# Latent attention: the values' low halves moved into one 128-column operand, the 64th added on VectorE

## The chip, the cores and the metric

One Trainium2 chip, one core. The metric is the device time of one execution in microseconds (us), median of several runs. The engines are TensorE (PE; its weight loads are shown apart as PEld), VectorE (DVE), ScalarE (ACT), GpSimd (POOL) and SyncE (SP), which issues the DMAs.

## The reference

Two layers on x of 1 x 512 x 1024 float32. In each, one projection of the normed input gives the inputs of three branches and three gates; the branches are projected, gated, summed and projected once more; a gated MLP with a depthwise convolution follows. The change is in branch A, the multi-head latent attention (MLA), with a few edits elsewhere:

```python
kv = (rms_norm(c_kv, kv_norm_g) @ w_ukv).reshape(b, s, MLA_HEADS, MLA_NOPE + MLA_V)
k_nope, v = kv[..., :MLA_NOPE], kv[..., MLA_NOPE:]      # MLA_V = 64, MLA_HEADS = 8
...
sc = jnp.einsum('bqgrd,bkgd->bgrqk', qi, k) * scale
p = jax.nn.softmax(sc, axis=-1)
return jnp.einsum('bgrqk,bkgv->bqgrv', p, v)
```

Branch B is a grouped-query attention (GQA) with 8 query and 2 key/value heads, branch C a multi-scale mean pooling.

## The kernel before, in words

**Numbers.** Every float32 operand of a matmul is held as a high and a low half of type float32r: `hi` is the rounded value (a copy on ACT or DVE), `lo` the difference (a subtraction on DVE or POOL). `mm3` (L351) multiplies hi·hi, lo·hi and hi·lo, three matmuls; all matmuls are issued by `mm` (L343, shown as L344) and all transposes by `turn` (L348). The moving operand has 512 columns, the 512 tokens, nearly everywhere. Weights stream from HBM in pieces (`w_dma` by SP, L298); `w_split` (L305) makes the halves `wh` (ACT) and `wl` (DVE or POOL).

**Order.** The program emits each engine's instructions in one written order. A planner, class `Clock`, keeps a modelled time: `chain` (L167) strings the steps that follow a PSUM result (copy, subtraction, release of the bank), each emitted when the model says that it is due; helper methods of class `Engine` carry a cost for it (L202 to L243, which is why most DVE, ACT and POOL instructions show those lines). `free(tag)` gives a PSUM bank back. The banks are named acc (2), S (1), ST (2), AV (2) and mi (1). An engine works strictly in order, so that an instruction whose input is late holds all behind it.

**Attention** (L1037), for GQA and then MLA, goes over 8 heads h with 4 key blocks k of 128 keys. `s_max` gives one score matmul per block into S, from which DVE reduces the negative maxima `nm`; `m_row` turns these into a row. `probs` computes the scores again into an ST bank (three matmuls in MLA), transposed with the maximum subtracted; ACT takes the exponential in place, ACT or DVE copies the high half `ph`, DVE subtracts the low half `pl` and then frees ST. `av_hi` multiplies the values with `ph` and `av_lo` with `pl` into an AV bank over the four blocks. The value operand `vmh` has 128 columns for each head: 64 high halves and 64 ones, so that rows 64 to 127 of AV hold the softmax's sum; the low halves `vml`, 64 columns, are a second matmul with `ph` in `av_hi`. `o_out` (L1203) copies the sum (`osum`) and the product (`oraw`) out; for every second head it turns the sums (`otr`), takes the reciprocal (`oinv`), spreads it, multiplies and splits into `oh` and `ol`, on POOL but for the last pair (h = 7), where DVE does it.

A table `PLAN` gives each step a position; between steps `Filler` units of three matmuls are emitted, as many as the position wants and up to `SLACK` = 35 more while a step's inputs or bank aren't ready. In the MLA stage the fillers are the gate and projection of branch B (`gates(1, ...)`) and then units of branch A's gates (`fc`, 16 of them in `beside`, L1292); the rest of `fc` runs behind the stage (`fc.finish()`). `_order(br)` (L57) lists the units of a branch: gate columns g, the projection b of the same columns `lag` steps later, and for branches 1 and 2 the making of MLA's queries, keys and values (`EXTRA`). `v_out` (L1011) writes the values of four heads and two blocks: high halves by `copy`, low halves on DVE from the acc bank, which is then freed. In each layer it runs four times, twice ahead of the MLA stage (heads 0 to 3) and twice in it (heads 4 to 7).

**Elsewhere touched**: `tok_major` (L548), the first projection, whose pieces each serve four blocks of tokens; the call of `norm_finish` in layer 0 (L661), which computes the norm's statistics on PE between units of the pooling projection; and `t_pair` of GQA, which turns query heads and splits them (`qa`, `qb`).

Of the kernel before, what the change touches and what calls it, by code (L numbers as in the profile page):

```python
# [38 lines left out]
SLACK = 35  # L39
PLAN = {"gqa": (0.006, 0.786, 0.986, 0.65, 3.252, 2.411, 4.57, 32.003),  # L40
        "mla": (-2.351, 0.028, 1.098, 0.64, 3.303, 1.678, 1.82, 33.91)}
W_BIAS = 2.54
C_BIAS = 0.2

# [12 lines left out]
def _order(br):  # L57


    r, lag = [], 2 if br == 0 else 1  # L60
    for m in range(KC + lag):
        r += [(k, pos.index(m)) for k, b, pos in EXTRA if b == br and m in pos]
        if m < KC:
            r.append(("g", m))
        if m >= lag:
            r.append(("b", m - lag))
    return r
# [120 lines left out]
class Engine:  # L188
# [33 lines left out]
        self._two(in_)  # L222
        return self.eng.tensor_reduce(out, in_, *a, **k)  # L223

    def tensor_scalar(self, out, *a):
        self._count(out, *((0.0043, 0.2) if self.kind == "Pool" else (0.00055, 0.07)))
        return self.eng.tensor_scalar(out, *a)

    def tensor_copy(self, out, in_, psum=False):
# [17 lines left out]
def trunk(ctx: ExitStack, tc: tile.TileContext, x, w, prm, gb, cst, out):  # L247
# [41 lines left out]
    def f(ap):  # L289
        return ap.bitcast(F32)  # L290
# [14 lines left out]
    def w_split():  # L305
        j = st["split"]
        sl, off, wd = pieces[j]
        r = raws[sl][:, off:off + wd]
        hi = hlp.tile([P, T], F32R, tag="wh", name=f"wh{j}")
        lo = hlp.tile([P, T], F32R, tag="wl", name=f"wl{j}")  # L310
        ck.fin = ck.now
        A.activation(hi[:, :wd], r, AF.Copy)
        e = V if j < KC + 3 else pick(W_BIAS, ck.fin + ck.SEM)
        ck.free[e.kind] = max(ck.free.get(e.kind, 0.0), ck.fin + ck.SEM)
        e.tensor_tensor(lo[:, :wd], r, f(hi[:, :wd]), ALU.subtract)
        done("w", j)
        halves[j] = (hi, lo)
        st["split"] += 1
# [44 lines left out]
    ident = C[:, C_ID:C_ID + P]  # L363
    ones = cp.tile([P, P], F32R, tag="ones", name="ones")
    mhalf = cp.tile([P, 1], F32, tag="mhalf", name="mhalf")


    MQ, MK = [[cp.tile([P, 4, 4, 96], F32, tag=f"{n}{g}", name=f"{n}{g}") for g in range(2)] for n in ("MQ", "MK")]
# [141 lines left out]
    def layer(l, sq, xsrc):  # L510
# [37 lines left out]
        def tok_major(banks, wd, between=None):  # L548
            for kc in range(KC):
                if between and kc == 4:  # L550
                    between()
                wh, wl = wnext()
                need(("H", G1, kc))
                for b in range(4):
                    bs = slice(b * P, b * P + P)
                    mm3(banks[b][:, :wd], HH[:, kc, bs], HL[:, kc, bs], wh[:, :wd], wl[:, :wd],
                        kc == 0, kc == KC - 1)
# [100 lines left out]
        for g in range(4):  # L658
            acc = ps(ptags[g])
            for n, _ in enumerate(feat_major(acc, G1)):  # L660
                if l == 0 and g == 0 and n == 3:  # L661
                    norm_finish(G1, sq, nrm)
                    latents()
            if g == (l == 0):
                norm_rows(G1, nrm, "acc")
            chain(*pool_steps(g, acc, ptags[g]))
# [218 lines left out]

        mla_make = {}
        VM = {}
        ss = small("ssm", [P, 2, 2, 4, 4])
        krr = small("krr", [P, 4, 32], bufs=1)
        kj_ = small("kj", [P, 4, 32], bufs=1)  # L890
# [118 lines left out]
                v_out(g, p, acc)  # L1009

        def v_out(g, p, acc):  # L1011
            lo2 = slot("vml", F32R)
            vs = []
            for i in range(2):
                v = slot("vmh", F32R)
                vh = v[:, :T].rearrange("p (h f) -> p h f", f=P)
                lv = lo2[:, 256 * i:256 * i + 256].rearrange("p (h f) -> p h f", f=64)
                G.memset(f(vh[:, :, 64:P]), 1.0)
                VM[2 * p + i, g] = (vh, lv)
                vs.append((vh[:, :, 0:64], lv, acc[:, 256 * i:256 * i + 256].rearrange("p (h f) -> p h f", f=64)))  # L1020

            def hi():
                for vh, _, src in vs:
                    copy(vh, src)

            def lo():
                for vh, lv, src in vs:
                    V.tensor_tensor(lv, src, f(vh), ALU.subtract)
                free("acc")
                done("vm", l, 2 * p, g)  # L1030
                done("vm", l, 2 * p + 1, g)
            chain(hi, lo)
# [4 lines left out]
        def attention(kind, fill, okey, odst):  # L1037
# [4 lines left out]
            def key(*k):  # L1042
                return (kind, l) + k
# [21 lines left out]
            def t_pair(h):  # L1065

                tp = ps("mi")
                for b in range(4):
                    need(("gqn", l, b))
                    turn(tp[:, b * P:b * P + P], gqo[b][:, 64 * h:64 * h + P])  # L1070
                need(("kab", l))
                steps = []
                for i in range(2):
                    s = hs[h + i] = {}
                    s["ka"], s["kb"] = KAB[h // 4]
                    qa, qb = s["qa"], s["qb"] = slot("qa", F32R), slot("qb", F32R)
                    own, other = slice(64 * i, 64 * i + 64), slice(64 - 64 * i, P - 64 * i)

                    def hi(qa=qa, own=own):
                        copy(qa[own, :T], tp[own])  # L1080

                    def lo(i=i, qa=qa, qb=qb, own=own, other=other):
                        V.tensor_tensor(qa[other, :T], tp[own], f(qa[own, :T]), ALU.subtract)
                        if i == 1:
                            free("mi")
                        A.activation(qb[0:64, :T], qa[own, :T], AF.Copy)
                        done(*key("q", h + i))

                    steps.append((hi, lo))
                chain(steps[0][0], steps[1][0], steps[0][1], steps[1][1])  # L1090
# [53 lines left out]
            def probs(h, k):  # L1144
# [22 lines left out]

                def lo():
                    V.tensor_tensor(pl[:, :T], sc, f(ph[:, :T]), ALU.subtract)
                    free("ST")  # L1170
                    done(*key("pl", h, k))

                chain(ex, hi, lo)

            def vals(h, k):
                if gqa:
                    need(("vg", l, k))
                    vh, vl = VG[k]
                    return vh[:, h // 4, :], vl[:, h // 4, :]
                need(("vm", l, k, h // 4))  # L1180
                vh, vl = VM[k, h // 4]
                return vh[:, h % 4, :], vl[:, h % 4, :]

            def av_hi(h, k):
                s = hs[h]
                need(key("ph", h, k))
                if k == 0:
                    s["av"] = ps("AV")
                vh, vl = vals(h, k)
                ph = s["p", k][0]  # L1190
                mm(s["av"], vh, ph[:, :T], k == 0, False)
                mm(s["av"][0:64], vl, ph[:, :T], False, False)

            def av_lo(h, k):
                s = hs[h]
                need(key("pl", h, k))
                vh, vl = vals(h, k)
                pl = s.pop(("p", k))[1]
                mm(s["av"], vh, pl[:, :T], False, k == 3)
                if k == 3:  # L1200
                    o_out(h)

            def o_out(h):  # L1203
                s = hs.pop(h)
# [5 lines left out]
                def copies():  # L1210
                    A.activation(sums[js, :T], s["av"][64:128], AF.Copy)
                    A.activation(raw[js, :T], s["av"][0:64], AF.Copy)
                    free("AV")

                steps = [copies]
                if h % 2 == 1:
                    oh, ol = slot("oh", F32R), slot("ol", F32R)
# [1 line left out]

                    turned, inv = slot("otr"), small("oinv", [P, 16])  # L1220
                    steps += [lambda: V.transpose(turned[:, :T], sums[:, :T]),
                              lambda: V.reciprocal(inv, turned[:, :T].rearrange("p (b f) -> p b f", f=32)[:, :, 0]),
                              lambda: V.transpose(sums[:, :T].rearrange("p (b f) -> p b f", f=32),
                                                  bc(inv.unsqueeze(2), [P, 16, 32]))]
                    steps += [lambda: (V if h == 7 else G).tensor_tensor(raw[:, :T], raw[:, :T], sums[:, :T], ALU.mult),
                              *split(oh[:, :T], ol[:, :T], raw[:, :T], eng=V if h == 7 else G),
# [5 lines left out]
            for h in range(8):  # L1232
                p0 = 4.0 * (h - 1)
                plan += [(p0 + tq, t_q, (h,)), (p0 + tk, t_k, (h,)),
                         (p0 + mr, m_row, (h,))]
                for k in range(4):
                    plan += [(p0 + s0 + ds * k, s_max, (h, k)), (p0 + 4 + k, probs, (h, k)),
                             (p0 + 4 + k + ah, av_hi, (h, k)), (p0 + 4 + k + al, av_lo, (h, k))]
            plan.sort(key=lambda z: z[0])

            def stretch(p):
# [2 lines left out]
            def waits(fn, h, k=None):  # L1244
# [10 lines left out]
                    return [key("m", h), key("q", h)] + [key("kl", h)] * (not gqa), "ST"  # L1255
                if fn is av_hi:
                    return [key("ph", h, k)], "AV" if k == 0 else None
                return [key("pl", h, k)] * (fn is av_lo), None

            def waiting(fn, *args):  # L1260
                keys, tag = waits(fn, *args)
# [30 lines left out]
        def beside():  # L1292

            yield from gates(1, "og", ogqa, "add")
            for _ in range(2 * KC):
                fc.step()
                yield

        fb = Filler(beside(), units(1) + 2 * KC)
        fb.upto(PRE_B)  # L1300
        while not ck.has(("mq", l, 0)) and fb.step():
            pass
# [128 lines left out]
    V.memset(warm, 0.0)  # L1431
    A.activation(warm, warm, AF.Exp)
    V.memset(f(ones), 1.0)
    idle = ps("mi")
    for _ in range(9):
        PE.matmul(idle, lhsT=ones, rhs=ones[:, None, :].to_broadcast([P, 4, P]), start=True, stop=True)
# [162 lines left out]
```

## Time and profile before

| what | value |
|---|---|
| median of 3 runs | 1649.69 us (1648.71 to 1650.75) |
| the profiled execution's own time | 1649.25 us |
| its span in the profile | 1647.3 us |
| instructions | 20363 |
| HBM read | 139.90 MB |
| mean DMA rate | 88 GB/s |

The profile shows one execution. "Busy" is the time in which an engine had an instruction at work. A group's row reads: line, engine, operation, output<-inputs by the program's names, sizes (partitions x elements), count | busy us, mean ns of one | idle us of the engine just before them, and what ended most of it. A row of the waits reads: who waited, for what, us in total, times, the longest. A row of a timeline reads: start, length (both us), engine, line, operation; in brackets the idle time ahead of it and what ended it. Matmuls overlap in the pipeline (a length of 0.40 us, but a start every 0.23 us); a slot is the time from one start to the next.

### The profile page before, as it was taken

How to read it: one execution, taken by the hardware profiler on the slowest of the kernel's cores; microseconds unless marked ns; L12 is line 12 of the kernel's file. 1: busy time of each engine (PE TensorE's matmuls, PEld its weight loads, DVE VectorE, ACT ScalarE, POOL GpSimd, SP SyncE). 2: the span in 40 equal slices, each digit the busy share in tenths (PEclk: the TensorE clock that was granted, in tenths of full speed). 3: DMA queues.
4: the chain of work that ended last, by engine and by line, in shares of the span. 5: the costliest groups of instructions: out<-in, count | busy, mean ns of one | idle time of the engine just before them, and what ended most of it. 6: DMA issues, size and time to landing. Idle time of an engine off the chain costs nothing.

```text
span 1647.3 us, 20363 instructions
## 1 busy us (share of the span) xinstructions
PE 1640.4 (100%) x7435; PEld 1336.7 (81%) x7435; DVE 890.5 (54%) x1404; ACT 761.8 (46%) x1357; POOL 921.9 (56%) x805
## 2 busy tenths in 40 slices
PE   9999999999999999999999999999999999999999
PEld 8887887778888888888888888877788888888888
DVE  6777756643366666621046677566332666666000
ACT  6457745543444444432244577455434444444221
POOL 3762763344666666654568538534446656656542
PEclk9999999999999999999999999999999999999999
DMA  5221121123322323333332211211243232332331
GB/s 201 82 84 46 60 65 48 52 71 118 119 90 90 103 90 91 102 102 122 102 103 89 82 39 62 74 39 52 85 133 95 85 103 90 91 101 90 126 111 45
DMA packets 44739, 145.40 MB, mean 88 GB/s; under 512 B 5088, under 2 KB 6624, under 8 KB 44640
## 3 DMA queue, kind: packets, MB, share of 16 engines
q1 hardware_dynamic: 44352, 143.97, 27.6%
q8 instruction: 59, 0.97, 0.2%
q14 instruction: 40, 0.33, 0.1%
q10 hardware_dynamic: 288, 0.14, 0.0%
HBM read 139.90 MB, written 4.19 MB: 87 GB/s over the span
## 4 chain that ended last, share of the span: by engine, by line
PE 98%; DVE 1%; ACT 1%; DMA 0%; SPq 0%; issue 0%
PE ps_acc L344 44%; PE ps_AV L344 24%; PE ps_ST L344 23%; PE ps_S L344 4%; PE ps_mi L344 2%; PE ps_mi L348 1%; DVE sq L215 0%; DMA XM<-x 0%; ACT wh L208 0%; ACT sqt L208 0%; DVE wl L215 0%; PE ps_acc L348 0%; SPq L301 0%; ACT HH L208 0%; SPq L1439 0%
## 5 line engine op out<-in xcount | busy, mean ns | idle before, releaser
L215 POOL TENSOR_TENSOR wl<-raw,wh 128x512 fp32r<-128x512 f32 (+2 forms) x508 | 662.9, 1315 | 589.0 <-ACT wh L208 457.7
L208 ACT ACTIVATE wh<-raw 128x512 fp32r<-128x512 f32 (+3 forms) x522 | 308.8, 607 | 125.6 <-PE ps_ST L344 41.1
L219 DVE SCALAR_TENSOR_TENSOR a<-u,prm,a 128x512 f32<-128x512 f32 x176 | 238.9, 1358 | 79.4 <-ACT a L208 73.2
L344 PE MATMUL ps_acc<-HH,wh 128*128 128x512 f32 x592 | 234.7, 396 | 1.4 <-DVE XM L219 1.4
L344 PE MATMUL ps_acc<-HL,wh 128*128 128x512 f32 x592 | 234.6, 396 | 0.0
L344 PE MATMUL ps_acc<-HH,wl 128*128 128x512 f32 x592 | 234.2, 396 | 0.0
L344 PEld LDWEIGHTS ps_acc<-HH,wh 128*128 128x128 f32 x592 | 111.5, 188 | 28.5 <-ACT mqs L208 1.7
L344 PEld LDWEIGHTS ps_acc<-HH,wl 128*128 128x128 f32 x592 | 111.3, 188 | 26.3
L344 PEld LDWEIGHTS ps_acc<-HL,wh 128*128 128x128 f32 x592 | 111.5, 188 | 25.5
L208 ACT ACTIVATE ps_ST<-ps_ST 128x512 f32<-128x512 f32 x128 | 74.6, 583 | 113.5 <-PE ps_ST L344 113.0
L344 PE MATMUL ps_AV<-HL,wh 128*128 128x512 f32 x288 | 114.2, 396 | 0.0
L344 PE MATMUL ps_AV<-HH,wl 128*128 128x512 f32 x288 | 114.2, 396 | 0.0
L344 PE MATMUL ps_AV<-HH,wh 128*128 128x512 f32 x288 | 113.6, 394 | 0.0
L223 DVE TENSOR_REDUCE nm<-ps_S 128x1 fp32r<-128x512 f32 x128 | 87.8, 686 | 42.4 <-PE ps_S L344 41.1
L215 DVE TENSOR_TENSOR pl<-ps_ST,ph 128x512 fp32r<-128x512 f32 x128 | 87.7, 685 | 38.4 <-ACT ph L208 37.4
L215 POOL TENSOR_TENSOR al<-a,ah 128x512 fp32r<-128x512 f32 x44 | 58.2, 1322 | 84.9 <-ACT ah L208 58.6
L344 PE MATMUL ps_ST<-HL,wh 128*128 128x512 f32 x240 | 95.3, 397 | 0.0
L344 PE MATMUL ps_ST<-HH,wl 128*128 128x512 f32 x240 | 95.0, 396 | 0.0
L344 PE MATMUL ps_ST<-HH,wh 128*128 128x512 f32 x240 | 94.6, 394 | 0.0
L208 ACT ACTIVATE a<-u,prm 128x512 f32<-128x512 f32 x88 | 71.8, 815 | 33.4 <-DVE u L215 33.4
L208 ACT ACTIVATE ah<-a 128x512 fp32r<-128x512 f32 x44 | 27.8, 631 | 116.0 <-DVE u L243 110.6
L208 ACT ACTIVATE a<-a 128x512 f32<-128x512 f32 x44 | 27.8, 632 | 113.0 <-DVE u L243 113.0
(361 smaller groups left out, 3543.8 us busy)
## 6 DMA issues: line engine op xcount, KB each, us to landing
raw<-w SPq DMA_DIRECT2D x228, 512.0 KB, 3.5
raw<-w SPq DMA_DIRECT2D x13, 384.0 KB, 3.1
XM<-x SPq DMA_DIRECT2D x16, 256.0 KB, 4.1
raw<-w SPq DMA_DIRECT2D x6, 448.0 KB, 3.4
xsp<-XM SPq DMA_DIRECT2D x8, 256.0 KB, 2.0
XM<-xsp SPq DMA_DIRECT2D x8, 256.0 KB, 3.4
out<-XM SPq DMA_DIRECT2D x7, 256.0 KB, 2.1
raw<-w SPq DMA_DIRECT2D x4, 432.0 KB, 3.1
```

What stands on the lines that cost most here:

```text
L208: return self.eng.activation(out, in_, func, **k)
L215: return self.eng.tensor_tensor(out, *a)
L219: return self.eng.scalar_tensor_tensor(out, *a)
L223: return self.eng.tensor_reduce(out, in_, *a, **k)
L344: PE.matmul(o, lhsT=lhsT, rhs=rhs, start=start, stop=stop)
L348: PE.transpose(o, src, ident)
```

## The change

- The value operand of a head, now `vm`, has 64 high halves, a single column of ones, and the low halves of columns 1 to 63. One matmul with `ph` gives the product of the high halves (rows 0 to 63 of AV), the sum (row 64) and 63 columns of the low product (rows 65 to 127). The second matmul of `av_hi` goes in MLA.
- The low half of column 0 (`vm0`, one number per key) is multiplied on DVE: the new step `rest` in `probs` makes `vt` = scores' exponentials x `vm0` for k = 0 and adds to it in place for k = 1 to 3. It runs after `pl`, and ST is freed after it. A new step `av_rest` per head multiplies `vt` with `unit` (ones in column 0, else zeros), which sums it over the keys into row 0 of AV. `PLAN` places it with `REST`.
- `o_out` in MLA, per pair of heads: two memsets clear the two sum rows in `osum`, one addition puts the low products on `oraw` (POOL, or DVE for h = 7), and two small copies on ACT spread the reciprocals to the partitions of the low rows.
- `_order(0)` has lag 3 for 2, and `beside` takes 24 units of `fc` for 16. The weights are packed in the same changed order.
- The first weight piece is used in the order high·high for the four blocks, low·high for the four, high·low for the four; its high half is copied on DVE instead of ACT.
- `norm_finish` of layer 0 is called after six units of the pooling projection instead of four.
- The high half of GQA's `t_pair` is always copied on ACT, where `copy` chose before.
- The planner's cost of a DVE tensor_scalar that reads PSUM is given.

```diff
+REST = 0.4
...
-    r, lag = [], 2 if br == 0 else 1
+    r, lag = [], 3 if br == 0 else 1
...
-    def tensor_scalar(self, out, *a):
-        self._count(out, *((0.0043, 0.2) if self.kind == "Pool" else (0.00055, 0.07)))
+    def tensor_scalar(self, out, *a, psum=False):
+        self._count(out, *((0.0043, 0.2) if self.kind == "Pool" else (0.00105 if psum else 0.00055, 0.07)))
...
-        A.activation(hi[:, :wd], r, AF.Copy)
+        if j == 0:
+            V.tensor_copy(hi[:, :wd], r)
+        else:
+            A.activation(hi[:, :wd], r, AF.Copy)
...
+                if st["use"] == 1:
+                    for n, (x_, w_) in enumerate(((HH, wh), (HL, wh), (HH, wl))):
+                        for b in range(4):
+                            mm(banks[b][:, :wd], x_[:, kc, b * P:b * P + P], w_[:, :wd], n == 0, False)
+                    continue
...
-                if l == 0 and g == 0 and n == 3:
+                if l == 0 and g == 0 and n == 5:
                     norm_finish(G1, sq, nrm)
...
         def v_out(g, p, acc):
-            lo2 = slot("vml", F32R)
...
-                v = slot("vmh", F32R)
+                b = 2 * p + i
+                v = slot("vm", F32R)
                 vh = v[:, :T].rearrange("p (h f) -> p h f", f=P)
-                G.memset(f(vh[:, :, 64:P]), 1.0)
+                G.memset(f(vh[:, :, 64:65]), 1.0)
+                v0 = vm0[:, b, 4 * g:4 * g + 4]
...
-                for vh, lv, src in vs:
-                    V.tensor_tensor(lv, src, f(vh), ALU.subtract)
+                for vh, v0, src in vs:
+                    V.tensor_tensor(vh[:, :, 65:P], src[:, :, 1:64], f(vh[:, :, 1:64]), ALU.subtract)
+                for vh, v0, src in vs:
+                    V.tensor_tensor(v0, src[:, :, 0], f(vh[:, :, 0]), ALU.subtract)
                 free("acc")
...
                     def hi(qa=qa, own=own):
-                        copy(qa[own, :T], tp[own])
+                        A.activation(qa[own, :T], tp[own], AF.Copy)
...
                 def lo():
                     V.tensor_tensor(pl[:, :T], sc, f(ph[:, :T]), ALU.subtract)
+                    done(*key("pl", h, k))
+                    if gqa:
+                        free("ST")
+
+                def rest():
+
+                    if k == 0:
+                        s["t"] = slot("vt", F32R)
+                        V.tensor_scalar(s["t"][:, :T], sc, vals(h, k)[1], None, ALU.mult, psum=True)
+                    else:
+                        t = s["t"][:, :T]
+                        V.scalar_tensor_tensor(t, sc, vals(h, k)[1], f(t),
+                                               ALU.mult, ALU.add)
                     free("ST")
-                    done(*key("pl", h, k))
-
-                chain(ex, hi, lo)
+                    if k == 3:
+                        done(*key("t", h))
+
+                chain(ex, hi, lo, *[([("vm", l, k, h // 4)], rest)] * (not gqa))
...
-                mm(s["av"][0:64], vl, ph[:, :T], False, False)
+                if gqa:
+                    mm(s["av"][0:64], vl, ph[:, :T], False, False)
...
+            def av_rest(h):
+                s = hs[h]
+                need(key("t", h))
+                mm(s["av"], unit, s["t"][:, :T], False, True)
+                o_out(h)
...
+                def add():
+
+                    for j in (0, 64):
+                        G.memset(sums[j:j + 1, :T], 0.0)
+                    (V if h == 7 else G).tensor_tensor(raw[:, :T], raw[:, :T], sums[:, :T], ALU.add)
...
+                    if not gqa:
+                        steps += [add, lambda: (A.activation(inv[32:64], inv[0:32], AF.Copy),
+                                                A.activation(inv[96:128], inv[64:96], AF.Copy))]
...
+                if not gqa:
+                    plan.append((p0 + 7 + al + REST, av_rest, (h,)))
...
-            for _ in range(2 * KC):
+            for _ in range(3 * KC):
                 fc.step()
                 yield
 
-        fb = Filler(beside(), units(1) + 2 * KC)
+        fb = Filler(beside(), units(1) + 3 * KC)
```

More of the change, by code (lines that the diff above doesn't have):

```diff
@@ L365, in trunk @@
     mhalf = cp.tile([P, 1], F32, tag="mhalf", name="mhalf")
+    unit = cp.tile([P, P], F32R, tag="unit", name="unit")
     MQ, MK = [[cp.tile([P, 4, 4, 96], F32, tag=f"{n}{g}", name=f"{n}{g}") for g in range(2)] for n in ("MQ", "MK")]
@@ L887, in layer @@
         VM = {}
+        vm0 = small("vm0", [P, 4, 8])
         ss = small("ssm", [P, 2, 2, 4, 4])
@@ L1011, in v_out @@
         def v_out(g, p, acc):
-            lo2 = slot("vml", F32R)
             vs = []
             for i in range(2):
-                v = slot("vmh", F32R)
+                b = 2 * p + i
+                v = slot("vm", F32R)
                 vh = v[:, :T].rearrange("p (h f) -> p h f", f=P)
-                lv = lo2[:, 256 * i:256 * i + 256].rearrange("p (h f) -> p h f", f=64)
-                G.memset(f(vh[:, :, 64:P]), 1.0)
-                VM[2 * p + i, g] = (vh, lv)
-                vs.append((vh[:, :, 0:64], lv, acc[:, 256 * i:256 * i + 256].rearrange("p (h f) -> p h f", f=64)))
+                G.memset(f(vh[:, :, 64:65]), 1.0)
+                v0 = vm0[:, b, 4 * g:4 * g + 4]
+                VM[b, g] = (vh, v0)
+                vs.append((vh, v0, acc[:, 256 * i:256 * i + 256].rearrange("p (h f) -> p h f", f=64)))
             def hi():
                 for vh, _, src in vs:
-                    copy(vh, src)
+                    copy(vh[:, :, 0:64], src)
             def lo():
-                for vh, lv, src in vs:
-                    V.tensor_tensor(lv, src, f(vh), ALU.subtract)
+                for vh, v0, src in vs:
+                    V.tensor_tensor(vh[:, :, 65:P], src[:, :, 1:64], f(vh[:, :, 1:64]), ALU.subtract)
+                for vh, v0, src in vs:
+                    V.tensor_tensor(v0, src[:, :, 0], f(vh[:, :, 0]), ALU.subtract)
                 free("acc")
@@ L1180, in vals @@
                 need(("vm", l, k, h // 4))
-                vh, vl = VM[k, h // 4]
-                return vh[:, h % 4, :], vl[:, h % 4, :]
+                vh, v0 = VM[k, h // 4]
+                return vh[:, h % 4, :], v0[:, h % 4:h % 4 + 1]
             def av_hi(h, k):
@@ L1198, in av_lo @@
                 pl = s.pop(("p", k))[1]
-                mm(s["av"], vh, pl[:, :T], False, k == 3)
-                if k == 3:
+                mm(s["av"], vh, pl[:, :T], False, gqa and k == 3)
+                if gqa and k == 3:
                     o_out(h)
+            def av_rest(h):
[3 more added lines that the diff above has]
+                o_out(h)
             def o_out(h):
@@ L1221, in o_out @@
                     steps += [lambda: V.transpose(turned[:, :T], sums[:, :T]),
-                              lambda: V.reciprocal(inv, turned[:, :T].rearrange("p (b f) -> p b f", f=32)[:, :, 0]),
-                              lambda: V.transpose(sums[:, :T].rearrange("p (b f) -> p b f", f=32),
+                              lambda: V.reciprocal(inv, turned[:, :T].rearrange("p (b f) -> p b f", f=32)[:, :, 0])]
+                    if not gqa:
+                        steps += [add, lambda: (A.activation(inv[32:64], inv[0:32], AF.Copy),
+                                                A.activation(inv[96:128], inv[64:96], AF.Copy))]
+                    steps += [lambda: V.transpose(sums[:, :T].rearrange("p (b f) -> p b f", f=32),
                                                   bc(inv.unsqueeze(2), [P, 16, 32]))]
@@ L1257, in waits @@
                     return [key("ph", h, k)], "AV" if k == 0 else None
-                return [key("pl", h, k)] * (fn is av_lo), None
+                return [key("t", h)] if fn is av_rest else [key("pl", h, k)], None
             def waiting(fn, *args):
@@ L1433, in trunk @@
     V.memset(f(ones), 1.0)
+    G.memset(f(unit), 0.0)
+    G.memset(f(unit[:, 0:1]), 1.0)
     idle = ps("mi")
```

## The prediction

> **What bounds the kernel now.** I read the page first (busy time of each engine, the forty slices, the shares of the chain that ended last), then PE's waits, then that chain in order of time.
>
> ```profile
> span 1647.3 us, 20363 instructions
> PE 1640.4 (100%) x7435; PEld 1336.7 (81%) x7435; DVE 890.5 (54%) x1404; ACT 761.8 (46%) x1357; POOL 921.9 (56%) x805
> PEclk9999999999999999999999999999999999999999
> PE 98%; DVE 1%; ACT 1%; DMA 0%; SPq 0%; issue 0%
> ```
> ```profile
> PE ps_acc L344 <- DVE XM L219: 1.4, 1, 1.4
> PE ps_mi L1436 <- DVE ones L243: 1.1, 1, 1.1
> PE ps_S L344 <- DVE sq L215: 0.6, 1, 0.6
> PE ps_acc L344 <- DVE vml L215: 0.4, 2, 0.2
> PE ps_acc L344 <- DVE wl L215: 0.2, 1, 0.2
> ```
>
> TensorE is busy all the span, with the full clock granted in every slice, and the chain is 98% TensorE. It is idle 1647.3 - 1640.4 = 6.9 us; the waits name 3.7 us of that. So a matmul taken out shortens the run by its slot, unless a wait appears; waits can give back 3.7 us at most. What a slot is, the chain in order of time shows where nothing interrupts it.
>
> ```profile
> 86.77 11.20 PE ps_AV L344 x48
> 353.89 63.27 PE ps_acc L344 x273
> ```
>
> 11.20 / 48 = 0.2333 and 63.27 / 273 = 0.2318 us: I take 0.2325 us for a matmul of 512 columns.
>
> **The change part by part.**
>
> *The matmuls.* Per head and key block the low-value matmul goes: 8 x 4 x 2 layers = 64. Per head one `unit` matmul comes: 16. Is the removed one, with 64 stationary columns, worth a full slot? The timeline of PE around one:
>
> ```profile
> 346.97 0.40 PE L344 MATMUL ps_AV<-ph,vml 128*64 128x512 f32 x1
> 347.21 0.40 PE L344 MATMUL ps_acc<-HH,wh 128*128 128x512 f32 x1
> ```
>
> From its start to the start of the next, an ordinary one, is 0.24 us: a full slot. Term 1: -48 x 0.2325 = **-11.2 us**.
>
> Its weight load is shorter, as the loads of the tile and the costliest groups show:
>
> ```profile
> L344 PEld LDWEIGHTS ps_AV<-ph,vml x64: 133/138/139, 244.0 to 1170.4; 128*64 128x64 f32 x64
> ```
> ```profile
> L344 PEld LDWEIGHTS ps_acc<-HH,wh 128*128 128x128 f32 x592 | 111.5, 188 | 28.5 <-ACT mqs L208 1.7
> ```
>
> If load time set the slot, 138/188 of one would go: 64 x 0.73 - 16 = 31 slots, -7.2 us. The equal spacing above speaks against that. [...]
>
> *The work on VectorE inside the latent-attention stage.* Per head and block one step more, `vt`: 32 a layer, PSUM in, a scalar per partition, from the second block on its own output as second input. No such step is in the trace; the nearest rows, from the groups with shapes kept apart and one small form from its tile's view:
>
> ```profile
> L219 DVE SCALAR_TENSOR_TENSOR a<-u,prm,a 128x512 f32<-128x512 f32 x176 | 238.9, 1358 | 79.4 <-ACT a L208 73.2 <-POOL wl L215 2.9
> L215 DVE TENSOR_TENSOR pl<-ps_ST,ph 128x512 fp32r<-128x512 f32 x128 | 87.7, 685 | 38.4 <-ACT ph L208 37.4
> L219 DVE SCALAR_TENSOR_TENSOR qb<-ps_mi,gcol,qa 96x512 fp32r<-96x512 f32 x16 | 11.6, 726 | 12.2 <-ACT qa L208 12.2
> L215 DVE TENSOR_TENSOR vml<-ps_acc,vmh 128x256 fp32r<-128x256 f32 x16 | 6.0, 416 | 0.8 <-ACT vmh L208 0.5 <-PE ps_acc L344 0.3
> ```
> ```profile
> L227 DVE TENSOR_SCALAR rt<-ps_S x4: 167/167/168, 27.3 to 1280.3; 128x8 f32<-128x8 f32 x4
> ```
>
> The bounds are 0.69 (`pl`) and 1.36 us (`a`, both tensors in SBUF). `qb` has the same form as `vt`: one tensor from PSUM, one from SBUF, a pointer scalar. So I take 0.72. A stage has 32 x 0.72 = 23.0 us of it and 4 x 0.17 = 0.7 us of new small subtractions (63 columns instead of 64 in the old ones cost nothing; the values of the first four heads are made ahead of the stage, as now). VectorE's load against the stage, by the windows (length, then PE, PEld, DVE, ACT, POOL):
>
> ```profile
> 228.00:354.00 126.00, 126.00 (x585) 100.45 (x584) 79.11 (x127) 68.05 (x124) 54.42 (x51) 1.00 0.17 51
> ```
>
> 79.1 + 23.0 + 0.7 = 102.8 of about 126 us: 82%, up from 63%. The stage itself keeps its length, since -24 matmuls (-5.6 us) are balanced by the eight gate units (24 matmuls) that `3*KC` pulls in; those are gone behind the stage, so the move is 0 in sum. Queued behind `vt` on VectorE are the next `nm`, `pl` and `qb`: a later `nm` keeps the one S bank longer, and ST is now freed by `vt` rather than `pl`, 0.7 us later. With two ST banks and the fillers between (up to 35 units early), I walked head 1 and the last head through by the order of instructions with these durations: PE finds every bank free, by 0.15 us at the tightest. I put 0 here, and the rival below for what I did not walk.
>
> *First values of a layer.* PE already waits there:
>
> ```profile
> 215.72 0.75 DVE L215 TENSOR_TENSOR vml<-ps_acc,vmh 128x256 fp32r<-128x256 f32 x2
> 216.02 0.39 PE L344 MATMUL ps_acc<-HH,wl 128*128 128x512 f32 x1
> 216.62 0.36 PE L344 MATMUL ps_acc<-wh,cth 128*128 128x256 f32 x1 [0.20 <-DVE vml L215]
> ```
>
> The bank comes free after two more small subtractions: 2 x 0.16. Term 2: **+0.3 a layer, +0.6**.
>
> *Second values of a layer.* In before, VectorE and PE run:
>
> ```profile
> 244.57 0.67 DVE L215 TENSOR_TENSOR pl<-ps_ST,ph 128x512 fp32r<-128x512 f32 x1
> 245.17 0.74 DVE L215 TENSOR_TENSOR vml<-ps_acc,vmh 128x256 fp32r<-128x256 f32 x2
> ...
> 246.98 0.28 PE L344 MATMUL ps_acc<-wh,cth 128*128 128x256 f32 x1
> ```
>
> In the changed order three ST matmuls that stood ahead of 246.98 stand behind it (their bank now waits for `vt`), and one `vml` matmul is gone: PE comes to that bank at 246.98 - 4 x 0.2325 = 246.05. VectorE does `vt` after `pl` (245.17 to 245.85), the two subtractions (to 246.6), the two small ones (to 246.93). PE goes on at about 247.0. Term 3: a new wait of 0.95 us, also at the same place of layer 1: **+1.9**.
>
> *Statistics of layer 0 at n==5.*
>
> ```profile
> 25.17 0.40 PE L344 MATMUL ps_AV<-HH,wl 128*128 128x512 f32 x1
> 26.18 1.05 PE L344 MATMUL ps_S<-ones,sq 128*128 128x2 f32 x8 [0.61 <-DVE sq L215]
> ...
> 35.57 0.39 PE L344 MATMUL ps_acc<-dgh,ones 128*128 128x512 f32 x1
> ```
>
> PE could have gone on at 25.40; now six matmuls (1.39 us) come first and reach to 26.79, past 26.18. The gap of 26.18 - 25.40 = 0.78 goes, by the profile's count 0.6. What is late next is the chain from these statistics to `dgh`, 9.4 us later on PE; it ends some 3 us before it is used, and starts only 26.79 - 26.18 = 0.6 us later. Term 4: **-0.7**.
>
> *Query halves on ScalarE.* The one long wait in the list ends with this queue:
>
> ```profile
> 148.04 0.69 DVE L231 CAST qa<-ps_mi 64x512 fp32r<-64x512 f32 x1 [0.71 <-ACT qa L208]
> ...
> 150.94 0.69 DVE L219 SCALAR_TENSOR_TENSOR XM<-gt,ps_acc 128x512 f32<-128x512 f32 x1
> ```
> ```profile
> 151.78 0.47 PE L344 MATMUL ps_acc<-HH,wh 128*128 128x512 f32 x1 [1.44 <-DVE XM L219]
> ```
>
> Without the cast VectorE's queue stands 0.7 to 1.0 us earlier (the cast and part of the idle time ahead of it); `XM` then ends at about 150.7 and PE goes on near 150.8. Next late is still `XM`, by about 0.5 us. Term 5: **-0.95**.
>
> *At nothing.* First weight piece: four HH products cover the low half, now behind a cast on VectorE; the second piece's low half is the later one in both. `o_out` per pair gets two one-row memsets and an addition on POOL, two small copies on ACT:
>
> ```profile
> L243 POOL MEMSET kh<- 4x512 f32 x16 | 8.3, 520 | 0.9
> L215 POOL TENSOR_TENSOR oraw<-oraw,osum 128x512 f32<-128x512 f32 x12 | 15.6, 1297 | 7.1 <-DVE osum L239 6.9
> ```
>
> That is 2 x 0.52 + 1.30 us on a POOL that is 43% busy (54.42 of 126). Only the last pair is awaited soon; its addition is VectorE's (0.69), so 1.04 + 0.69 us and two small copies, an estimated 2.3 us more. Now its low half is ready at 359.52 and used at 363.74:
>
> ```profile
> 358.83 0.69 DVE L215 TENSOR_TENSOR ol<-oraw,oh 128x512 fp32r<-128x512 f32 x1 [0.70 <-ACT oh L208]
> ```
> ```profile
> 363.74 0.39 PE L344 MATMUL ps_acc<-ol,wh 128*128 128x512 f32 x1
> ```
>
> 4.2 us of cover; `lag` 3 puts one gate (24 matmuls, 5.6 us) more ahead of the use and the moved units take as much away. Some 2 us are left. If that cover fails, up to 2.3 us a layer come back. The weights' stream keeps its amount, only its order changes: no DMA is added.
>
> **Sum:** -11.2 + 0.6 + 1.9 - 0.7 - 0.95 = -10.35 us. The profiled execution takes 1649.25 us (span 1647.3 and 1.95 around it), 0.44 below the median 1649.69 of the runs: 1638.9 there, **1639.3** for the median.
>
> **The rivals.**
>
> A. *VectorE is late more often in the stage* (82%, in order, ST freed 0.7 us later). For it: at the one place where I found a wait it is 0.95 us; against it: the walked heads had none. If three to four of the six heads I did not walk have one of 0.5 to 1 us in both layers, 2 x 1.5 to 2 x 3.5 us: 1642 to 1646, most likely 1644.
>
> B. *`vt` costs as `a<-u,prm,a`, slower than before.* Then the stage's VectorE has 79.1 + 32 x 1.36 + 0.7 = 123 of 126 us, in order and with dependencies that leave it idle 37% now. Each block grows by 0.64 us, 32 x 0.64 = 20.5 us a layer; if the idle 23 us take half, +10 us a layer: 1639 + 20 = 1659. It decides from about 1.05 us a step: half of 32 x 0.33 us, twice, is the whole gain. Against it: `qb`, 726 ns while POOL works. [...]
>
> C. *The 64-column matmul gives back only its load's share*: -7.2 for -11.2, 1643.3. Against it the spacing.
>
> D. *The new waits don't come* (VectorE's queue ahead at the value sites): terms 2 and 3 gone, 1636.8.
>
> **How the numbers follow.** Forecast 0.60 (1637.5 to 1642), A 0.22, D 0.08, B 0.07, C 0.03. A measurement of this kernel can tell about 0.2%, 3.3 us, from no change: faster is under 1646.4, slower over 1653.0. Within it lies only A's upper end with part of B's lower, 0.03. Faster 0.90, same 0.03, slower 0.07. The range 1636.5 to 1645.0 leaves out B (0.07), A's upper end (0.06) and some of D (0.03).
>
> **What would show it.** In the changed profile: 7387 matmuls; `vt` near 0.72 us; VectorE about 103 us in the stage's windows; PE's waits on `XM` down to 0.5 us, none on `sq`, two on the small value subtractions of the first site (0.5 each) and two of about 0.9 in the stage. Many waits on `vt`, `nm` or ST in the list would be A, a `vt` above 1 us B, a chain with slots unlike 0.2325 us C. I am wrong if PE's idle time grows by more than 3 us, or if the last pair's longer chain makes PE wait behind a stage.

## The result and the profile after

| | median, us | runs | against before, with the 95% interval |
|---|---|---|---|
| before | 1649.51 | 1648.71 to 1650.75 | |
| changed | 1637.84 | 1637.68 to 1638.13 | 0.9931 (0.9918 to 0.9943) |

The forecast was 1639.3 in a range of 1636.5 to 1645.0. The profiled execution of the changed kernel took 1637.68 us, 11.57 less than that of before; the sum had said 10.35. The page of the changed kernel, then PE's waits (for what, us in total, times, longest):

```profile
span 1635.8 us, 20398 instructions
PE 1628.8 (100%) x7387; PEld 1329.2 (81%) x7387; DVE 935.4 (57%) x1485; ACT 767.1 (47%) x1374; POOL 935.9 (57%) x829
PE 98%; DVE 1%; ACT 0%; DMA 0%; issue 0%
```
```profile
PE ps_acc L348 <- DVE vm L216: 1.9, 4, 0.6
PE ps_mi L1484 <- DVE ones L244: 1.1, 1, 1.1
PE ps_acc L348 <- DVE XM L220: 0.5, 1, 0.5
PE ps_acc L348 <- DVE wh L232: 0.4, 1, 0.4
```

48 matmuls are gone. TensorE's idle time, 1635.8 - 1628.8 = 7.0 us, is what it was (6.9): the waits on `sq` and `XM` went down by 1.5 us and those on the small value subtractions up by 1.5. The tile view of `vt` and the window of the latent-attention stage (length, then PE, PEld, DVE, ACT, POOL):

```profile
L220 DVE SCALAR_TENSOR_TENSOR vt<-ps_ST,vm,vt x48: 659/742/753, 246.4 to 1164.2; 128x512 fp32r<-128x512 f32 x48
L228 DVE TENSOR_SCALAR vt<-ps_ST,vm x16: 736/737/743, 243.7 to 1158.3; 128x512 fp32r<-128x512 f32 x16
```
```profile
226.00:352.00 126.00, 125.40 (x580) 101.00 (x579) 99.56 (x165) 71.41 (x132) 61.61 (x62) 1.00 0.18 55
```

`vt` takes 0.74 us, and VectorE is busy 99.6 of 126 us (79%; the prediction had 102.8).

Where the time went is read from places that both chains of work show in order of time. Of the changed kernel:

```profile
85.95 11.21 PE ps_AV L348 x48
215.01 10.05 PE ps_acc L348 x45
697.81 15.21 PE ps_acc L348 x66
899.19 11.20 PE ps_AV L348 x48
1027.53 10.05 PE ps_acc L348 x45
1510.15 15.28 PE ps_acc L348 x66
```

and of before, where the prediction has not shown them (its 86.77 is the first):

```profile
216.62 10.05 PE ps_acc L344 x45
703.89 15.27 PE ps_acc L344 x66
905.77 11.20 PE ps_AV L344 x48
1034.14 10.06 PE ps_acc L344 x45
1521.70 15.27 PE ps_acc L344 x66
```

The lead at these places is 0.82, 1.61, 6.08, 6.58, 6.61 and 11.55 us. So the start gives 0.82, the grouped-query stage of layer 0 with the first values 0.79, the latent-attention stage with what follows it up to the MLP 4.47 and 4.94 in the two layers. The 0.50 between 703.89 and 905.77 is the gated MLP: eight groups of 66 matmuls at 15.20 us in place of 15.26. No edit touches them, other executions below have 15.20 or 15.29 there, and this small difference stays unexplained.

### The profile page after: what moved, and what is told of

Same layout as the page of the kernel before. It is cut to its first block, busy times and chain, and to the rows that moved or that the text cites. A ratio compares the mean times of both kernels' runs of the same rounds, so it can differ in the third digit from the quotient of the medians.

```text
span 1635.8 us, 20398 instructions
## 1 busy us (share of the span) xinstructions
PE 1628.8 (100%) x7387; PEld 1329.2 (81%) x7387; DVE 935.4 (57%) x1485; ACT 767.1 (47%) x1374; POOL 935.9 (57%) x829
## 4 chain that ended last, share of the span: by engine, by line
PE 98%; DVE 1%; ACT 0%; DMA 0%; issue 0%
PE ps_acc L348 44%; PE ps_AV L348 24%; PE ps_ST L348 24%; PE ps_S L348 4%; PE ps_mi L348 2%; PE ps_mi L352 1%; DVE vm L216 0%; DMA prm<-prm 0%; DVE pl L216 0%; ACT ps_ST L209 0%; PE ps_acc L352 0%; DVE vm L232 0%; DVE ph L232 0%; DVE nm L224 0%; DVE vt L228 0%
## 5 line engine op out<-in xcount | busy, mean ns | idle before, releaser
L209 ACT ACTIVATE wh<-raw 128x512 fp32r<-128x512 f32 (+1 forms) x521 | 308.9, 608 | 126.6 <-PE ps_ST L348 42.2
L216 DVE TENSOR_TENSOR pl<-ps_ST,ph 128x512 fp32r<-128x512 f32 x128 | 87.5, 684 | 25.3 <-ACT ph L209 24.3
```

What stands on the lines that cost most here:

```text
L209: return self.eng.activation(out, in_, func, **k)
L216: return self.eng.tensor_tensor(out, *a)
```

## The experiments

**Theory:** the time is the sum of slots and waits, -11.2 us of matmuls and four small terms, with `lag` and the moved units at nothing. **Rival:** the matmuls can only be saved while TensorE has other work between the steps of a stage that now asks more of VectorE; the moved units and `lag` are what pays.

Each run stands against executions of before taken beside it (medians 1648.89 to 1649.18, where 1649.51 stands above). "The changed kernel" is 1637.84 us throughout, so a difference to it is good to about 0.6 us.

**The value parts alone.** All other edits undone in the changed kernel:

```diff
-    r, lag = [], 3 if br == 0 else 1
+    r, lag = [], 2 if br == 0 else 1
-            for _ in range(3 * KC):
+            for _ in range(2 * KC):
...
-                if l == 0 and g == 0 and n == 5:
+                if l == 0 and g == 0 and n == 3:
-                        A.activation(qa[own, :T], tp[own], AF.Copy)
+                        copy(qa[own, :T], tp[own])
```
and the first weight piece as before.

> The changed kernel with only the value operand, vt, the unit matmul and the longer output chain; lag, 24 units, the first weight piece, the sixth unit for the statistics and the query halves are as before. Theory (sum of terms): -48 slots of 0.2325 us and two kinds of value waits, measured +0.14 and +0.6 us a layer in the changed kernel: -11.2 + 1.5 = -9.7 us against before, with the waits on XM (1.4) and sq (0.6) back in the list. Rival (the other edits carry part of the gain: without lag 3 the last pair's longer chain makes TensorE wait behind the stage): up to 2.3 us a layer less, so -5 to -8 us, with a wait on ol in the list.

Measured: 1650.28 us (1648.75 to 1655.24), 1.0006 of before (0.9997 to 1.0016). The whole gain is gone: 48 matmuls fewer, and the same time. The theory said 1639.8; even the rival's price, up to 2.3 us a layer, is too low. PE at the end of the stage of layer 0:

```profile
353.98 0.50 PE L345 MATMUL ps_ST<-qa,kl 96*128 96x512 f32 x1 [0.42 <-DVE vt L220]
...
356.24 0.51 PE L345 MATMUL ps_AV<-ph,vm 128*128 128x512 f32 x1 [0.44 <-ACT ph L209]
356.97 0.69 PE L345 MATMUL ps_AV<-pl,vm 128*128 128x512 f32 x1 [0.22 <-DVE pl L216]
357.63 0.80 PE L345 MATMUL ps_AV<-vt,unit 128*128 128x512 f32 x1
358.22 0.63 PE L345 MATMUL ps_acc<-HH,wh 128*128 128x512 f32 x1
358.65 0.63 PE L345 MATMUL ps_acc<-HL,wh 128*128 128x512 f32 x1
```

TensorE has no units left to put between these steps. It follows the last head's chain of ScalarE and VectorE, with starts 0.6 to 0.9 us apart; then it runs ordinary matmuls 0.43 us apart, not 0.23, at a granted clock of 0.50 (358 to 360 us). (This profiled execution, 1655.24 us, is the highest of its ten: it also lost some 4 us at the start of layer 0, where TensorE waited 2.1 us for `sq` and then ran at half clock for 3.4 us: the granted clock is 0.97 from 20 to 30 us and 0.86 from 30 to 40.) The places used above, in this execution:

```profile
220.53 10.03 PE ps_acc L345 x45
708.41 15.27 PE ps_acc L345 x66
1038.87 10.05 PE ps_acc L345 x45
1527.13 15.32 PE ps_acc L345 x66
```

From the first values to the MLP it takes 487.88 and 488.26 us in the two layers; before takes 487.27 and 487.56, the changed kernel 482.80 and 482.62. So 5.1 and 5.6 us are lost in this stretch, 10.7 of the 12.4 between the medians; the waits on `XM` and `sq` that come back are most of the rest.

**The other edits alone**, on the kernel before:

> The kernel before with only the other edits: lag 3 and 24 units, the first weight piece, the sixth unit, the query halves on ACT. Theory: the waits on XM (-0.95) and sq (-0.7) shrink, the first piece costs 0 to 0.1, lag and units give 0: -1.5 us against before. Rival (lag and units themselves help the stage): -3 us or more.

Measured: 1647.72 us against 1649.16, -1.4 us; ratio 0.9992 (0.9982 to 1.0001), so by timing alone not told from no change. In the list of waits `XM` is 0.5 and `sq` is missing, as forecast. Without the value parts, `lag` and the units give nothing: the stretch from the first values to the MLP takes 487.40 and 487.39 us, about what before takes. The two halves of the change are thus worth about +1.1 and -1.4 us alone, and -11.7 together.

**Which of the two edits.** The changed kernel with one of them undone:

```diff
-    r, lag = [], 3 if br == 0 else 1
+    r, lag = [], 2 if br == 0 else 1
```

> The changed kernel with lag 2 again and the 24 units kept in the stage. The first projection of branch A then follows the stage at once. Theory (the gate between the stage and the projection covers the last pair's chain, which the run with only the value parts shows to take 10.2 us from the unit matmul to the low half's use): nine matmuls, 2.1 us, are all the cover left, so a wait of about 8 us a layer on oh or ol, with a lower granted clock behind it: 1654 or more. Rival (lag is only an order): same as the changed kernel, 1638.

Measured: 1650.84 us (1650.45 to 1652.4), 1.0011 of before (1.0002 to 1.0021): 13.0 above the changed kernel, 6.5 a layer. The mechanism was as expected; the wait was half of the 8 us, so that 1654 was not reached: from the `unit` matmul to the first use of `oh` were 7.7 us (353.19 to 360.92), and 15 matmuls stood between, not nine. The timeline of PE, and the windows of two us (PEclk is the third number from the end):

```profile
356.69 0.40 PE L348 MATMUL ps_acc<-oh,wl 128*128 128x512 f32 x1
360.92 0.80 PE L348 MATMUL ps_acc<-oh,wh 128*128 128x512 f32 x1 [3.83 <-ACT oh L209]
361.65 0.80 PE L348 MATMUL ps_acc<-ol,wh 128*128 128x512 f32 x1
```
```profile
358.00:360.00 2.00, 0.00 (x0) 0.00 (x0) 1.86 (x3) 0.00 (x0) 0.00 (x0) 0.87 0.00 0
...
362.00:364.00 2.00, 2.00 (x6) 1.52 (x6) 1.06 (x2) 0.00 (x0) 0.79 (x1) 0.50 0.14 18
364.00:366.00 2.00, 2.00 (x6) 1.61 (x5) 1.01 (x2) 1.65 (x3) 0.42 (x1) 0.50 0.71 244
```

The wait is 4.0 us beyond a slot, 3.83 idle by the profile. Then there are six matmuls in two us where more than eight fit: at clock 0.50 the rest of the 6.5 us goes. The same with the units:

```diff
-            for _ in range(3 * KC):
+            for _ in range(2 * KC):
-        fb = Filler(beside(), units(1) + 3 * KC)
+        fb = Filler(beside(), units(1) + 2 * KC)
```

> The changed kernel with 16 units again and lag 3 kept. Theory (the eight units are what TensorE has between the steps of the last head; without them it waits in small pieces and the granted clock falls): about 4 to 5 us a layer, 1646 to 1648, with PE's waits on vt, ph and pl at the end of each stage and a granted clock under 1 there. Rival (the longer chain behind the stage was what the run with only the value parts lost): with lag 3 the chain is covered, 1638 to 1639.

Measured: 1643.93 us (1643.57 to 1645.77), 0.9968 of before (0.9957 to 0.9978): 6.1 above the changed kernel, half of its gain. The kind was as expected, the size a little under it. The stage's end in both layers, windows of two us:

```profile
348.00:350.00 2.00, 1.55 (x5) 0.86 (x5) 1.97 (x4) 1.23 (x4) 0.00 (x0) 1.00 0.00 0
350.00:352.00 2.00, 1.18 (x4) 0.40 (x3) 1.61 (x3) 1.06 (x2) 0.86 (x1) 1.00 0.00 0
352.00:354.00 2.00, 2.00 (x5) 1.57 (x6) 0.80 (x2) 1.41 (x3) 0.42 (x1) 0.58 0.00 0
354.00:356.00 2.00, 2.00 (x7) 1.55 (x6) 0.17 (x1) 1.46 (x4) 1.52 (x2) 0.57 0.00 0
...
1164.00:1166.00 2.00, 1.58 (x8) 0.95 (x7) 1.97 (x5) 1.12 (x2) 0.00 (x0) 1.00 0.00 0
1166.00:1168.00 2.00, 1.44 (x5) 0.53 (x3) 1.67 (x3) 1.58 (x3) 0.00 (x0) 1.00 0.00 0
1168.00:1170.00 2.00, 1.61 (x6) 1.01 (x6) 0.98 (x2) 0.55 (x2) 1.27 (x1) 1.00 0.00 0
```

In both layers the last 14 matmuls of the stage take 6.3 us (346.05 to 352.32, and 1163.12 to 1169.37) where 14 x 0.2325 = 3.3 would do: 3.0 us a layer. VectorE is busy meanwhile (1.97, then 1.61 of 2.00 in layer 0). In layer 0 the clock then falls for 3.4 us, some 1.5 us more; in layer 1, after nearly the same pattern, it does not. This execution took 1645.14 us; the median, 1.2 us lower, fits the waits of 2 x 3.0 us without the fall, but no trace of such an execution was kept.

**What `vt` costs.** Three edits of `rest`: `vt` made only for k = 0, a second such step into a scratch tile, and `vt` made from SBUF. The first:

```diff
-                    else:
-                        t = s["t"][:, :T]
-                        V.scalar_tensor_tensor(t, sc, vals(h, k)[1], f(t),
-                                               ALU.mult, ALU.add)
```

> The changed kernel with vt made only for the first key block of a head (the low halves of column 0 are left out for the three other blocks; the unit matmul stays). VectorE loses 48 x 0.74 us = 17.8 us a layer pair's 48 steps, 17.8 us a layer at 24 steps each. Theory (vt lies beside TensorE's work): within 0.7 us of the changed kernel, PE's waits unlike only at the value sites. Rival (vt holds ST banks and delays TensorE in small steps that no wait names): 2 us or more faster than the changed kernel.

Measured: 1636.86 us, 1.0 below the changed kernel. VectorE has 87.5 us in the stage in place of 99.6, and PE's wait on the value subtractions is 0.7 (2 times) in place of 1.9 (4 times): the second site's wait makes up the difference, a little more than the 0.7 us that the theory allowed. Elsewhere `vt` costs nothing, as it said. (The 17.8 us of the expectation are the 24 steps of one layer.) The second:

```diff
+                    if k == 0:
+                        s["x"] = slot("vx", F32R)
+                    x = s["x"][:, :T]
+                    V.scalar_tensor_tensor(x, sc, vals(h, k)[1], f(s["t"][:, :T]),
+                                           ALU.mult, ALU.add)
```

> The changed kernel with one more instruction like vt per head and key block into a scratch tile, ahead of the release of ST (nothing else reads it). VectorE in a latent-attention stage: 99.6 + 32 x 0.74 = 123 of about 126 us. Theory (an in-order engine near 100% makes TensorE wait at S, ST and the value sites; half of the added 23.7 us a layer shows): +10 us a layer, +20 us against the changed kernel, 1658. Rival (the fillers hide all up to a full VectorE): +0 to +4 us.

Measured: 1672.3 us, 34.5 above the changed kernel, where 20 was expected: 17.2 of the 23.7 us that VectorE gets more a layer. The windows at the end of the stage of layer 0:

```profile
350.00:354.00 4.00, 2.80 (x7) 1.26 (x7) 3.93 (x8) 1.87 (x6) 1.27 (x1) 0.84 0.00 0
354.00:358.00 4.00, 2.15 (x7) 1.64 (x7) 3.94 (x6) 1.19 (x2) 1.84 (x2) 0.50 0.00 0
```

Up to 338 us TensorE is at 100% but for the second value site; the loss is at the end, where VectorE is the one engine that is busy all the time and the clock halves. The third (the step for k = 0 is changed likewise, and ST is freed after `pl`):

```diff
-                        V.scalar_tensor_tensor(t, sc, vals(h, k)[1], f(t),
+                        V.scalar_tensor_tensor(t, f(ph[:, :T]), vals(h, k)[1], f(t),
                                                ALU.mult, ALU.add)
```

> The changed kernel with vt made from the high half ph in SBUF instead of the scores' bank (the low half of a probability times the low half of a value is left out), so that vt has two tensors in SBUF and ST is freed after pl, as in the kernel before. Theory (two SBUF inputs beside a working POOL cost as a<-u,prm,a): vt for the later blocks 1.2 to 1.5 us, VectorE 99.6 + 24 x 0.6 = 114 of 126 us in a stage, and 2 to 10 us slower than the changed kernel. Rival (where the tensor lies costs nothing): vt 0.7 to 0.75 us and, with ST free 0.7 us earlier, the same time or up to 1.2 us faster.

Measured: 1639.07 us, 1.2 above the changed kernel. The tile view:

```profile
L220 DVE SCALAR_TENSOR_TENSOR vt<-ph,vm,vt x48: 702/1000/1835, 246.0 to 1164.9; 128x512 fp32r<-128x512 f32 x48
```

From PSUM the step took 659 to 753 ns; with both tensors in SBUF it takes 702 to 1835, and VectorE has 108.7 us in the stage. That costs only 1.2 us, between the two: under the 2 of the theory, over the 0 of the rival. The likely reasons, not tested apart, are that ST is freed earlier and that 108.7 of 126 us still fits. What makes one step from SBUF take 702 ns and another 1835 was not shown. In the changed kernel, from PSUM, a tensor operation of POOL ran beside 32 of the 48 steps, and all 48 took 659 to 753; `a<-u,prm,a`, with both tensors in SBUF, took 750 to 1781 there.

**A slot.** A second matmul of 64 columns put back:

```diff
                 mm(s["av"], vh, ph[:, :T], k == 0, False)
+                if not gqa:
+                    mm(s["av"][0:64], vh[:, 0:64], ph[:, :T], False, False)
```

> The changed kernel with a second matmul of 64 stationary columns per head and key block put back (the high halves of the values once more on ph, so the output holds them twice); no VectorE work is added. Theory (a slot is 0.2325 us whatever the number of columns): +64 x 0.2325 = +14.9 us against the changed kernel, 1652.7. Rival (the shorter weight load sets the slot): 138/188 of a slot or less, +10.9 us or less.

Measured: 1653.04 us, 15.2 above the changed kernel: 15.2 / 64 = 0.2375 us. A matmul of 64 stationary columns cost a full slot here.

**The same in grouped-query attention.** If units are what limits the gain, the operand can serve there too.

> The changed kernel with the same value operand, vt and unit matmul in the grouped-query attention as well: 48 matmuls less again. VectorE in that stage: 83.3 + 32 x 0.74 + about 1 = 108 of 118 - 5.6 us. Theory (the gain is 48 slots less new waits at a VectorE that is 96% busy): -11.2 us and +2 to +8 us of waits, 1629 to 1635. Rival (VectorE bounds this stage): no faster than the changed kernel, 1638 or more.

Measured: 1645.57 us, slower than the changed kernel by 7.7, as the rival had it. But the waits lie at the end of that stage, after the units: PE is busy 2.56 of 4 us from 198 on. So a gate of branch A (its weights moved in the stream accordingly) was put there with `lag` 4, then two with 5, then three with 6; `lag` rises along, so that one gate still stands between the latent-attention stage and the first projection. With three:

```diff
+        def first():
+            yield from gates(2, "op", opool, "first")
+            for _ in range(3 * KC):
+                fc.step()
+                yield
-        fa = Filler(gates(2, "op", opool, "first"), units(2))
+        fa = Filler(first(), units(2) + 3 * KC)
```

> The version with the value operand in both attentions, and one gate of branch A (eight units) moved into the grouped-query stage as well, with lag 4, so that each stage keeps as many matmuls as in the kernel before. Theory (what the version without the units lost is the end of that stage, where TensorE ran out of units and the clock fell): -11.2 us against the changed kernel and +1 to +4 us of waits at a VectorE near 90%: 1628 to 1631. Rival (VectorE or the tiles' slots bound the stage): 1636 or more.

> The version with the value operand in both attentions, with two gates of branch A (16 units) in the grouped-query stage and lag 5. In the version with eight units TensorE waits 7.2 us between 204 and 220 us of the first layer, with VectorE busy all that time. Theory (missing units at that end): about half of those waits filled, 1634 to 1637. Rival (VectorE bounds that end; PE must wait for it wherever the units stand): within 1.5 us of the version with eight, 1638 to 1641.

> The same with three gates (24 units) and lag 6. Theory (missing units): most of the waits filled, 1629 to 1634, faster than the version with 16 units. Rival (VectorE bounds): no faster than the version with eight, 1638 to 1641.

| units of branch A in the grouped-query stage | median, us | against before |
|---|---|---|
| 0 | 1645.57 | 0.9980 (0.9971 to 0.9990) |
| 8 | 1639.63 | 0.9943 (0.9929 to 0.9958) |
| 16 | 1633.30 | 0.9905 (0.9891 to 0.9920) |
| 24 | 1629.56 | 0.9882 (0.9866 to 0.9899) |

Two readings in these expectations don't come out of the profiles. Without units the clock did not fall at that end in the profiled execution: it is 1.00 in all windows from 190 to 214 us. And of the 7.2 us with eight units the profile shows 3.1: TensorE is busy 12.88 of the 16 us.

With eight the rival's 1636 or more was measured, and VectorE, busy 3.97 of 4 us there, looked like the bound; 16 and 24 show that it was not: 1633.3 is a little under what missing units were to give, 1629.6 within it. With 24 units PE's waits are those of the changed kernel again, but for 0.6 us more on `XM`, and in 118 us of the grouped-query stage VectorE works 98:

```profile
90.00:208.00 118.00, 117.94 (x542) 96.28 (x541) 98.02 (x159) 78.16 (x146) 77.20 (x95) 1.00 0.21 68
```

This version beats both kernels: 8.3 us under the changed one, 19.3 under before.

## Why the prediction was right, and where it was not

- **Term 1 (-11.2) was right**: 48 slots, measured at 0.2375 us apiece in the other direction. Rival C is out.
- **Terms 2 and 3 (+2.5) had the right places and too large a size.** Beyond a slot, the gap at the first site went from 0.37 to 0.51 us (+0.14, forecast 0.3), the one at the second is 0.77 (forecast 0.95; the waits count 0.6). The term that was mis-sized is the small subtraction: I took its 0.17 us as its share, but four run into each other:

```profile
213.99 0.88 DVE L216 TENSOR_TENSOR vm<-ps_acc,vm 128x252 fp32r<-128x252 f32 x4
...
215.01 0.36 PE L348 MATMUL ps_acc<-wh,cth 128*128 128x256 f32 x1 [0.34 <-DVE vm L216]
```

  The two large ones alone took 0.75, so two small ones add 0.13. In both layers this makes 0.7 us of the 1.2 by which the sum fell short; the MLP's 0.5 is the rest. That holds for the total only. Place by place, 24 slots less 0.77 are 4.8 us a layer where the two stretches gave 4.47 and 4.94. Part of it is the slot itself, 57.22 / 246 = 0.2326 us from the end of that stage in layer 0, where before has 0.2318; why stays open.

```profile
353.98 57.22 PE ps_acc L348 x246
```
- **Terms 4 and 5 were right**: the lead is 0.82 us after the start (0.7, and the first weight piece at 0; its wait by the profile went from 0.2 to 0.4), and the wait on `XM` went from 1.4 to 0.5.
- **`vt` at 0.72 was right** (0.74), and so was 0 for it in the stage: the run with `vt` only once shows nothing but the second site. Rival B's condition did not hold; its price was too low, since doubling the step cost 34.5 us and not 20.
- **The step "the move is 0 in sum" gave the right time, but not for its reason.** The length of the stage did stay about as said, but I booked the 24 moved matmuls as a shift that neither gives nor costs, and put VectorE's other lateness in the stage at 0 beside it. That 0 holds only with them. They are the work that TensorE does while the last heads wait for VectorE: taken back, 6.1 us return, and without both edits the value parts gain nothing. Had the change lacked them, my way of summing would still have said -9.7. That the sum came out is in part luck.
- **"If that cover fails, up to 2.3 us a layer come back" was too small.** Without `lag` 3 it was 6.5 us. I counted only the lengthening. In the prediction's own terms, lag 2 takes the gate's 5.6 us off the 2 that are left, a wait of 3.6, and 4.0 was measured; the lower clock behind the wait was not in the sum. With `lag` 3, the "some 2 us" left were 1.0. Its low half is ready at 362.17, its use starts at 363.15:

```profile
358.32 0.69 DVE L216 TENSOR_TENSOR oraw<-oraw,osum 128x512 f32<-128x512 f32 x1 [2.04 <-POOL osum L244]
361.48 0.69 DVE L216 TENSOR_TENSOR ol<-oraw,oh 128x512 fp32r<-128x512 f32 x1 [0.76 <-ACT oh L209]
363.15 0.39 PE L348 MATMUL ps_acc<-ol,wh 128*128 128x512 f32 x1
```

  VectorE waited 2.04 us for the two memsets, which I had at 1.04: they took 1.09 together, but stood behind a weight split on POOL (from 355.96, 1.30 us).
- Rival A was not the case here, but with 16 units it is: small waits on ST, `ph` and `pl`, at the end of the stage and not at the heads in the middle that I had not walked.

## What to carry to other kernels

Here a matmul taken out of a stage was saved only while independent matmuls remained to put between its dependent steps (48 matmuls out gave 11.7 us with `lag` and the units, and nothing without); count them to the stage's very end, where they ran out first. A step "moved at no cost" should be priced by taking it back. And a wait of TensorE should be priced with the lower clock behind it, which added about half as much again where it fell (some 2.5 us to 4.0, and 1.5 to 3.0).

## What the runs showed of the hardware

After the wait of 4.0 us in the run with lag 2 the granted clock was 0.50 from 360 to 366 us (0.87 in the two us ahead, 0.92 in the two behind), and the starts of matmuls were 0.43 us apart where they are 0.23. By an estimate from the 0.87 it fell at about 359.5 us, 2.4 us into the wait.

Other waits differ in what followed:

- With only the value parts, the wait of 2.1 us at the start of layer 0 was followed by matmuls 0.43 us apart for some 3 us (29.81 to 32.79).
- In before, the wait of 1.4 us on `XM` was not: the clock was 1.00 from 148 to 156 us, though TensorE was busy for 0.56 of the two us from 150 to 152.
- In the run with 16 units the clock fell for 3.4 us in layer 0 with no gap between two starts above 0.93 us, TensorE being busy by the profile for 4.6 of 6 us (346 to 352). In layer 1 it was busy for 4.6 of 6 us as well (1164 to 1170), with a gap of 0.95 us, and the clock stayed at 1.00.

So neither the longest gap nor the busy share tells the two layers of that run apart. What decides it the runs did not show.
